# A top-256 search in an RWKV-7 and sparse-attention block: scratch room, conversions and fixed places for evictions

## The chip, the cores and the metric

The kernel runs on one core of a Trainium2 chip. A core has five engines that work side by side, each through its own queue in order: TensorE (PE, with its weight loads PEld), VectorE (DVE), ScalarE (ACT), GpSimd (POOL) and SyncE (SP), which issues the transfers. The metric is the device time of one execution in microseconds.

## The reference, cut to what matters

One block over T = 1024 tokens of width 1024. One projection of the normalised input feeds three parts: an RWKV-7 mixing, a sparse attention whose keys are picked by an indexer, and the gates that merge both; a feed-forward part follows. The change lies in the picking of the keys:

```
score  = einsum('bqh,bqhs->bqs', wi, relu(einsum('bqhd,bsd->bqhs', qi, ki)))
score  = where(causal, score, -inf)
_, idx = lax.top_k(score, 256)               # per query, over 1024 keys
s = where(valid, q . k[idx] / 8, -inf); p = softmax(s); out = p . v[idx]
z = token_shift(h @ w_in[rwkv columns], mu)  # z + (previous token's z - z) * mu
```

Queries go in eight blocks of 128. Blocks 0 and 1 have at most 256 keys and need no selection; block b has (b+1)*128 keys.

## The kernel before

The kernel has no gather. For each query it finds the 256th largest score exactly and writes a bias of 0 or -1e30 over the scores, which the attention adds. The scores are turned into integers of the same order and split into two int16 halves, `hi` and `lo`. `select` (L537 to L638) is a generator for three query blocks; two of them run, one for blocks 3, 4, 5 on ACT and one for blocks 2, 6, 7 on DVE, and L640 to L642 advance both in turn:

- *First half*: 16 steps of a bisection on `hi`. DVE (`bisect`) compares the 128 x n keys of each block with the candidate and counts in the same instruction, L577; two instructions of three columns make the next candidate. ACT (`bisect_signs`) takes the sign of key minus candidate and sums it, L590; POOL makes the next candidate, L592 to L598.
- *Conversion*, L605 to L615: `lo` becomes (hi - found) * 65536 + lo, clamped to int16. POOL does it for ACT's blocks (with a cast `low`), DVE for its own.
- *Second half*: the same 16 steps on the new `lo`.
- *Finals*, L616 to L638, on DVE for all six blocks: the threshold `thr`, `ge` (count), `eq`, a scan `cs` over the equal keys to break ties, two more passes and the bias.

The output of a comparison (`jk`) is junk; only its sum counts. These outputs and `q16`, `low`, `ge`, `eq`, `cs` and the attention's `hl` and `qs` all take slots of one ring of six tiles, tag `t4` (L352). A slot is free when the readers and writers of its last tenant are done, on whatever engine.

Beside the selection PE runs projections, each half (512 tokens) a run of 24 matmuls into a PSUM tile `dn` of a pool of two. First come the gates' (`gate1`, all pulled at L524, ACT evicts them at L452; the weights of the next unit are split by ACT L209 and POOL L210), then those of the RWKV part (`rin`): a half is 8 steps of that generator, and its eviction is a token shift by two engines: ACT L669 scales, DVE L670 adds the neighbour, ACT L673 or DVE L675 handles the column between the halves. 106 steps are pulled at L815 after the selection's code; then `q_split` makes `hl` (ACT L421, POOL L422) and PE transposes it (L430) for the first attention block, whose scores go through DVE at L774.

The order on each engine is made by a scheduler when the kernel is built: it goes by the program's order, dependencies and its own estimates. `after(first, ins)` (L175) adds a dependency that only fixes an order. So an eviction stands where the scheduler puts it between the comparisons.

Of the kernel before, what the change touches and what calls it, by code (L numbers as in the profile page):

```python
# [23 lines left out]
P = 128  # L24
# [9 lines left out]
NEG = -3.0e38  # L34
BIG = 1.0e30
PE_WINDOW = 32
FILL = [8, 2, 40, 3, 6, 22]
AHEAD = [6, 6, 6, 0, 0, 0, 0, 0, 1, 1, 0, 10]
FIN_LAG = 5
# [56 lines left out]
def hybrid_block(ctx: ExitStack, tc: tile.TileContext, a, out, dbg=None, stop=99):  # L96
# [78 lines left out]
    def after(first, ins):  # L175

        tc.add_manual_dep(ins.ins, first.ins.name, mybir.DependencyInfo(
            mybir.DependencyClass.NoSync, mybir.DependencyReason.DATA), reason="order of a queue")
# [20 lines left out]
    def pull(gen, n):  # L199
        for _ in range(n):  # L200
            if next(gen, "end") == "end":
                return
# [149 lines left out]
    def t4(name, dtype=F32):  # L352
        return dsa.tile([P, 1024], dtype, name=name, tag="t4", bufs=6)
# [176 lines left out]
    def t4b(name, n, dtype):  # L530
        return t4(name).bitcast(dtype)[:, 0:n]
# [5 lines left out]
    def select(blocks, act=False):  # L537
# [5 lines left out]
        def sm_(name, dtype=F32):  # L543
            return dsa.tile([P, m_], dtype, name=f"{name}{gi}")

        hi, lo = {}, {}
        room, o = None, 4096
        for b in reversed(blocks):
            n = (b + 1) * P
            if o + 2 * n > 4096:  # L550
                room, o = (key_room() if n > 384 else dsa.tile([P, 768], I16, name="room2")), 0
            hi[b], lo[b] = room[:, o:o + n], room[:, o + n:o + 2 * n]
            o += 2 * n
# [18 lines left out]
        def bisect(src):  # L572
            nc.vector.memset(cand, 0.0)
            for k in range(15, -1, -1):
                for j, b in enumerate(blocks):
                    junk = t4b("jk", (b + 1) * P, BF16)
                    nc.vector.tensor_scalar(junk, src[b], cand[:, j:j + 1], None, op0=OP.is_ge, op1=OP.add,  # L577
                                            accum_out=cnt[:, j:j + 1])
                up, down = step_of(k)
                nc.vector.tensor_scalar(ok, cnt, float(TOPK), up, op0=OP.is_ge, op1=OP.mult)  # L580
                nc.vector.scalar_tensor_tensor(cand, ok, -down, cand, op0=OP.add, op1=OP.add)
                yield

        def bisect_signs(src):
# [16 lines left out]

        search = bisect_signs if act else bisect
        yield from search(hi)
        th, tl = sm_("th"), sm_("tl", I32)
        eng.tensor_copy(th, cand)  # L605
        for j, b in enumerate(blocks):
            n = (b + 1) * P
            q = t4("q16")[:, 0:n]
            eng.tensor_scalar(q, hi[b], th[:, j:j + 1], 65536.0, op0=OP.subtract, op1=OP.mult)
            low = lo[b]  # L610
            if act:
                low = t4("low")[:, 0:n]
                eng.tensor_copy(low, lo[b])
            eng.tensor_tensor(q, q, low, op=OP.add)
            eng.tensor_scalar(lo[b], q, 32767.0, -32768.0, op0=OP.min, op1=OP.max)  # L615
        yield from search(lo)  # L616
        thr, ti = sm_("thr"), sm_("ti", I32)
        nc.vector.tensor_copy(ti, th)
        nc.vector.tensor_scalar(ti, ti, 16, None, op0=OP.logical_shift_left)
        nc.vector.tensor_scalar(tl, cand, 32768.0, None, op0=OP.add)  # L620
        nc.vector.tensor_tensor(ti, ti, tl, op=OP.bitwise_or)
# [15 lines left out]
            nc.vector.scalar_tensor_tensor(cs, sc[b], t_ap, cs, op0=OP.is_gt, op1=OP.add)  # L637
            nc.vector.tensor_scalar(sc[b], cs, BIG, -BIG, op0=OP.mult, op1=OP.add)  # L638

    searches = [select(blocks, act) for blocks, act in SELECT]  # L640
    while searches:
        searches = [g_ for g_ in searches if next(g_, "end") != "end"]  # L642
    if "bias" in dbg:
        for b in range(NB):
            nc.sync.dma_start(dbg["bias"][b * P:(b + 1) * P, 0:(b + 1) * P], sc[b])


    zd = dram.tile([4, P, 5, T], F32, name="zd")
# [13 lines left out]
    def shifted(c0, m, mkey, mi, fin):  # L662
        z = ev4()[0:m]
        last = base.tile([P, 1], F32, name="last", tag="last", bufs=2)[0:m]
        m0, m1 = pcol(mkey, mi)[0:m], pcol1(mkey, mi)[0:m]

        def evac(hf, ps):
            o = hf * 512
            nc.scalar.activation(z[:, o:o + 512], ps, AF.Copy, scale=m1)  # L669
            nc.vector.scalar_tensor_tensor(z[:, o + 1:o + 512], ps[:, 0:511], m0, z[:, o + 1:o + 512],  # L670
                                           op0=OP.mult, op1=OP.add)
            if hf == 0:
                nc.scalar.activation(last, ps[:, 511:512], AF.Copy)  # L673
            else:
                nc.vector.scalar_tensor_tensor(z[:, 512:513], last, m0, z[:, 512:513], op0=OP.mult, op1=OP.add)  # L675
                fin(z)

        yield from in_b(c0, m, evac)
# [7 lines left out]
    def split_lr(z, n):  # L686
        w = dsa.tile([P, 2, 1024], F32R, name="lrt", tag="room", bufs=2)
        nc.scalar.activation(w[0:n, 0, :], z, AF.Copy)
        nc.gpsimd.tensor_tensor(w[0:n, 1, :], z, w[0:n, 0, :].bitcast(F32), op=OP.subtract)
        return w  # L690

    def rwkv_in():
        keep = []
# [118 lines left out]
            nc.sync.dma_start(yt_dram[1, :, :, b * P:(b + 1) * P].rearrange("c p t -> p c t"), yT)  # L812

    rin = rwkv_in()
    pull(rin, RIN[0] - QF)  # L815
    A["hl"] = q_split(0, 0)
    pull(rin, QF)
    units = [(b, p) for b in range(NB) for p in range(4)]
# [774 lines left out]
    def in_order(ins):  # L1593
        if queue:
            after(queue[-1], ins)
        queue.append(ins)
# [154 lines left out]
```

## Time and profile before

| what | value |
|---|---|
| median of three runs | 1817.76 us (1809.3 to 1817.8) |
| profiled execution | 1819.81 us, span 1818.0 |
| mean granted TensorE clock | 0.959 |
| PE busy | 1697.3 us, 93% of the span |
| DVE busy | 1320.5 us, 73% |
| ACT, POOL busy | 895.2 us, 833.7 us |
| matmuls L189 into `dn` | 379.5 us in 1488 |
| DVE comparisons L577 | 92.6 us in 96, 15.1 idle before them |
| ACT comparisons L590 | 78.4 us in 96, 33.4 idle before them |

The profile follows one execution. Busy times are shares of the span of 1818.0 us; the profiled time has 1.8 us more. Times in the views count from the span's start; "A <- B" reads "A waited for B". A granted clock of 1.00 is 2.4 GHz, 0.50 is 1.2 GHz. Idle time of an engine costs only where something later waits for it.

### The profile page before, as it was taken

The numbers are of one execution on the slowest core, as the hardware profiler recorded it, in microseconds if no ns is written. First come the engines' busy times: TensorE is split into PE (matmuls) and PEld (weight loads), VectorE is DVE, ScalarE is ACT, GpSimd is POOL, SyncE is SP. The second block draws the span as 40 slices with busy tenths as digits, with TensorE's granted clock in tenths as the row PEclk, the third lists the DMA queues.
The fourth block names the chain that finished last, engine by engine and source line by source line (L and its number), as shares of the span: only waits on it lengthen the run. The fifth ranks groups of instructions, "written<-read, shape, count | busy, mean of one in ns | idle before, by whom it ended". The sixth has DMA issues, their size and how long they took to land.

```text
span 1818.0 us, 27188 instructions
## 1 busy us (share of the span) xinstructions
PE 1697.3 (93%) x9554; PEld 1424.4 (78%) x9554; DVE 1320.5 (73%) x2601; ACT 895.2 (49%) x1751; POOL 833.7 (46%) x761
## 2 busy tenths in 40 slices
PE   6999899849999999989898898999999999999997
PEld 6988887738788777777777797977888888888885
DVE  5689955996777454578666746699988875874988
ACT  5375664717777534245435425463444444444453
POOL 1522566324353334243423532286666656545552
PEclk9999999969999998799878999999999999999999
DMA  5230343212311355336436559415544549653444
GB/s 170 79 116 30 115 141 110 64 41 85 123 35 36 134 138 151 84 109 172 121 88 183 158 159 327 127 53 186 172 147 141 177 145 329 186 162 99 141 148 140
DMA packets 268287, 242.04 MB, mean 133 GB/s; under 512 B 64284, under 2 KB 206934, under 8 KB 268150
## 3 DMA queue, kind: packets, MB, share of 16 engines
q1 hardware_dynamic: 268150, 240.30, 42.3%
q8 instruction: 75, 1.23, 0.3%
q14 instruction: 62, 0.51, 0.1%
HBM read 164.76 MB, written 75.50 MB: 132 GB/s over the span
## 4 chain that ended last, share of the span: by engine, by line
PE 61%; DVE 18%; DMA 6%; POOL 4%; ACT 4%; issue 4%; SPq 1%; POOLq 0%; DVEq 0%; ACTq 0%
PE up L189 24%; PE dn L189 15%; PE sm L189 9%; DVE jk L577 3%; PE sm L192 2%; PE ch L189 2%; PE acc L189 2%; PE dn L243 1%; PE dn L244 1%; DVE w L1328 1%; PE dn L242 1%; DVE Zt L998 1%; PE acc L243 1%; POOL h L1328 1%; PE acc L242 1%
## 5 line engine op out<-in xcount | busy, mean ns | idle before, releaser
L189 PE MATMUL dn<-hT,w 128*128 128x512 f32 (+1 forms) x1488 | 379.5, 402 | 8.3 <-ACT last L673 7.5
L189 PEld LDWEIGHTS dn<-hT,w 128*128 128x128 f32 (+1 forms) x1488 | 274.0, 189 | 67.5 <-ACT last L673 10.1
L189 PE MATMUL up<-h,w 128*128 128x512 f32 x1344 | 312.1, 393 | 6.4 <-DVE w L1328 3.1
L189 PEld LDWEIGHTS up<-h,w 128*128 128x128 f32 x1344 | 252.3, 189 | 63.3 <-DVE w L1328 5.0
L1328 DVE TENSOR_TENSOR w<-st,w 128x512 fp32r<-128x512 f32 x216 | 213.5, 1022 | 75.6 <-ACT w L1327 75.5
L210 POOL TENSOR_TENSOR w<-st,w 128x1024 fp32r<-128x1024 f32 (+2 forms) x75 | 179.7, 2397 | 164.6 <-ACT w L209 139.1
L189 PE MATMUL up<-w 128*128 128x512 f32 x1008 | 246.1, 390 | 2.7 <-DVE w L1328 2.7
L189 PEld LDWEIGHTS up<-w 128*128 128x128 f32 x1008 | 188.6, 188 | 44.5 <-DVE w L1328 5.4
L1327 ACT ACTIVATE w<-st 128x512 fp32r<-128x512 f32 x216 | 127.9, 624 | 158.3 <-PE up L189 49.7
L1621 POOL TENSOR_TENSOR st<-wb,wb 128x512 f32<-128x512 f32 x80 | 120.7, 1512 | 93.9 <-DVE w L1328 73.8
L1483 POOL TENSOR_TENSOR c<-st 128x512 f32<-128x512 f32 x80 | 124.6, 1565 | 52.0 <-DMA st<-in_w_ffn_up 26.2
L209 ACT ACTIVATE w<-st 128x1024 fp32r<-128x1024 f32 (+2 forms) x91 | 94.7, 1041 | 42.0 <-PE acc L244 15.0
L577 DVE TENSOR_SCALAR_CACHE_REDUCE jk<-room,cand 128x384 bf16<-128x384 int16 (+2 forms) x96 | 92.6, 1008 | 15.1 <-ACT jk L590 14.1
L1494 POOL TENSOR_TENSOR C<-C 128x512 f32<-128x512 f32 x64 | 75.5, 1180 | 59.1 <-ACT C L1493 59.1
L243 PE MATMUL dn<-w,hT 128*128 128x256 f32 (+1 forms) x320 | 92.1, 289 | 6.3 <-DVE w L210 6.3
L780 POOL TENSOR_SCALAR sm<-sm,rs 128x128 f32<-128x128 f32 (+7 forms) x64 | 47.8, 748 | 105.1 <-DVE rs L779 55.2
L590 ACT ACTIVATE jk<-room,neg 128x512 bf16<-128x512 int16 (+2 forms) x96 | 78.4, 819 | 33.4 <-POOL neg L598 21.8
L242 PE MATMUL dn<-w,hT 128*128 128x256 f32 (+1 forms) x320 | 92.0, 290 | 0.9 <-ACT hT L272 0.9
L244 PE MATMUL dn<-w,hT 128*128 128x256 f32 (+1 forms) x320 | 92.0, 290 | 0.0
L1328 DVE TENSOR_TENSOR w<-c,w 128x512 fp32r<-128x512 f32 x80 | 82.7, 1046 | 0.4
L189 PE MATMUL sm<-w 128*128 128x512 f32 x288 | 81.1, 389 | 0.0
L1327 ACT ACTIVATE w<-c 128x512 fp32r<-128x512 f32 x80 | 48.8, 627 | 64.4 <-PE up L189 52.0
(336 smaller groups left out, 3546.3 us busy)
## 6 DMA issues: line engine op xcount, KB each, us to landing
st<-hcd SPq DMA_DIRECT2D x112, 256.0 KB
st<-in_w_in SPq DMA_DIRECT2D x54, 512.0 KB
st<-in_w_ffn_up SPq DMA_DIRECT2D x36, 512.0 KB
hcd<-C SPq DMA_DIRECT2D x16, 1024.0 KB
wb<-in_w_ffn_down SPq DMA_DIRECT2D x64, 256.0 KB
hcd<-kc SPq DMA_DIRECT2D x16, 768.0 KB
zd<-ev SPq DMA_DIRECT2D x20, 512.0 KB
gzd<-ev SPq DMA_DIRECT2D x32, 256.0 KB
```

The lines of the kernel that those rows point to most:

```text
L189: pe(nc.tensor.matmul(*args, **kw))
L209: nc.scalar.activation(hi, st[0:rows, 0:n], AF.Copy)
L210: (eng or nc.gpsimd).tensor_tensor(lo, st[0:rows, 0:n], hi.bitcast(F32), op=OP.subtract)
L242: nc.tensor.matmul(ps, l[0], r[0], start=start, stop=False, skip_group_check=shared)
L243: nc.tensor.matmul(ps, l[0], r[1], start=False, stop=False, skip_group_check=shared)
L244: nc.tensor.matmul(ps, l[1], r[0], start=False, stop=stop, skip_group_check=shared)
L577: nc.vector.tensor_scalar(junk, src[b], cand[:, j:j + 1], None, op0=OP.is_ge, op1=OP.add, accum_out=cnt[:, j:j + 1])
L590: nc.scalar.activation(junk, src[b], AF.Sign, bias=neg[:, j:j + 1], accum_out=cnt[:, j:j + 1])
L1327: nc.scalar.activation(hi, src, AF.Copy)
L1328: return eng.tensor_tensor(lo, src, hi.bitcast(F32), op=OP.subtract)
L1483: nc.gpsimd.tensor_tensor(c, src, blocks[LEFT[p][2]], op=OP.add if LEFT[p][1] == "+" else OP.subtract)
L1621: nc.gpsimd.tensor_tensor(c, src, wblocks[RIGHT[p][2], f], op=OP.add if RIGHT[p][1] == "+" else OP.subtract)
```

## The change

- DVE's comparisons get a tile of their own for their junk, outside the ring.
- Both conversions are on DVE; the cast `low` is dropped (DVE reads int16 directly).
- More `yield`s: DVE's second half stands in the program after both conversions.
- `in_order` ties DVE's first comparison of each step, its last instruction, the conversions, the finals' start and the evictions L670 (now L674) into one fixed order.
- The steps of `rin` are pulled in the selection's loop, by the numbers in `SPREAD`: eight (one half, one eviction) after each of eight turns of the second half, none after the others. The remaining 42 of the 106 follow after the loop.

```diff
+SPREAD = [0, 0, 0, 0, 0, 8, 8, 8, 8, 0, 8, 8, 8, 0, 8]
...
+        jk = None if act else dsa.tile([P, 1024], BF16, name="jk")
...
-                    junk = t4b("jk", (b + 1) * P, BF16)
-                    nc.vector.tensor_scalar(junk, src[b], cand[:, j:j + 1], None, op0=OP.is_ge, op1=OP.add,
-                                            accum_out=cnt[:, j:j + 1])
+                    ins = nc.vector.tensor_scalar(jk[:, 0:(b + 1) * P], src[b], cand[:, j:j + 1], None,
+                                                  op0=OP.is_ge, op1=OP.add, accum_out=cnt[:, j:j + 1])
+                    if j == 0:
+                        in_order(ins)
...
-                nc.vector.scalar_tensor_tensor(cand, ok, -down, cand, op0=OP.add, op1=OP.add)
+                own["V"] = nc.vector.scalar_tensor_tensor(cand, ok, -down, cand, op0=OP.add, op1=OP.add)
...
         yield from search(hi)
+        if act:
+            yield
...
-            eng.tensor_scalar(q, hi[b], th[:, j:j + 1], 65536.0, op0=OP.subtract, op1=OP.mult)
-            low = lo[b]
-            if act:
-                low = t4("low")[:, 0:n]
-                eng.tensor_copy(low, lo[b])
-            eng.tensor_tensor(q, q, low, op=OP.add)
-            eng.tensor_scalar(lo[b], q, 32767.0, -32768.0, op0=OP.min, op1=OP.max)
+            nc.vector.tensor_scalar(q, hi[b], th[:, j:j + 1], 65536.0, op0=OP.subtract, op1=OP.mult)
+            nc.vector.tensor_tensor(q, q, lo[b], op=OP.add)
+            own["V"] = in_order(nc.vector.tensor_scalar(lo[b], q, 32767.0, -32768.0, op0=OP.min, op1=OP.max))
+        if not act:
+            yield
         yield from search(lo)
         thr, ti = sm_("thr"), sm_("ti", I32)
-        nc.vector.tensor_copy(ti, th)
+        in_order(nc.vector.tensor_copy(ti, th))
...
+    own = {}
+
+    def in_order(ins):
+
+        if "V" in own:
+            after(own["V"], ins)
+        return ins
...
+            ins = in_order(nc.vector.scalar_tensor_tensor(z[:, o + 1:o + 512], ps[:, 0:511], m0,
+                                                          z[:, o + 1:o + 512], op0=OP.mult, op1=OP.add))
+            if searching[0]:
+                own["V"] = ins
...
     rin = rwkv_in()
-    pull(rin, RIN[0] - QF)
+    searches = [select(blocks, act) for blocks, act in SELECT]
+    searching[0], turn, early = True, 0, 0
+    while searches:
+        searches = [g_ for g_ in searches if next(g_, "end") != "end"]
+        n_ = SPREAD[turn - 19] if 19 <= turn < 19 + len(SPREAD) else 0
+        pull(rin, n_)
+        early += n_
+        turn += 1
+    searching[0] = False
...
+    pull(rin, RIN[0] - QF - early)
```

Where the order moves, first on ACT at the end of the first half. `jk` is a comparison, `ev` the eviction of a gate's half, `w` a weight split. Before, the last two steps and what follows:

```order
L590 ACTIVATE jk,cnt_2712<-room,neg_2716 128x512
L590 ACTIVATE jk,cnt_2712<-room,neg_2716 128x640
L452 ACTIVATE ev<-dn 128x512
L209 ACTIVATE w<-st 128x1024
L590 ACTIVATE jk,cnt_2712<-room,neg_2716 128x768
L452 ACTIVATE ev<-dn 128x512
L209 ACTIVATE w<-st 128x1024
L590 ACTIVATE jk,cnt_2712<-room,neg_2716 128x512
L590 ACTIVATE jk,cnt_2712<-room,neg_2716 128x640
L590 ACTIVATE jk,cnt_2712<-room,neg_2716 128x768
L452 ACTIVATE ev<-dn 128x512
L209 ACTIVATE w<-st 128x1024
```

After, the last two steps (lines are numbered as in the changed kernel; L452, L209 and L590 are now L453, L210 and L593):

```order
L593 ACTIVATE jk,cnt_2715<-room,neg_2719 128x512
L593 ACTIVATE jk,cnt_2715<-room,neg_2719 128x640
L593 ACTIVATE jk,cnt_2715<-room,neg_2719 128x768
L593 ACTIVATE jk,cnt_2715<-room,neg_2719 128x512
L593 ACTIVATE jk,cnt_2715<-room,neg_2719 128x640
L453 ACTIVATE ev<-dn 128x512
L210 ACTIVATE w<-st 128x1024
L593 ACTIVATE jk,cnt_2715<-room,neg_2719 128x768
L453 ACTIVATE ev<-dn 128x512
L210 ACTIVATE w<-st 128x1024
L453 ACTIVATE ev<-dn 128x512
L210 ACTIVATE w<-st 128x1024
```

Counted from the search's start, the evictions in the first piece are the eighth, ninth and tenth, those in the second the seventh to ninth: the sixteenth step's last comparison stands behind the ninth before and behind the seventh now. Four more gate evictions stand ahead of the second half before; now two do, and four stand within it.

On DVE, from the last step of the first half to the second half (`th` the found value, `q` the conversion, `room` the halves). Before, where the cast of `th_3031` is that of ACT's blocks, which DVE needs for the finals only:

```order
L581 SCALAR_TENSOR_TENSOR cand_2738<-ok_2739,cand_2738 128x3
L605 COPY th_3063<-cand_2738 128x3
L573 MEMSET cand_2738 128x3
L618 CAST ti_3398<-th_3063 128x3
L619 TENSOR_SCALAR ti_3398<-ti_3398 128x3
L618 CAST ti_3359<-th_3031 128x3
L619 TENSOR_SCALAR ti_3359<-ti_3359 128x3
L670 SCALAR_TENSOR_TENSOR ev<-dn,par,ev 128x511
L609 TENSOR_SCALAR q_3066<-room_2721,th_3063 128x384
L609 TENSOR_SCALAR q_3070<-room,th_3063 128x896
L609 TENSOR_SCALAR q_3074<-room,th_3063 128x1024
L614 TENSOR_TENSOR q_3066<-q_3066,room_2721 128x384
```

After, the end of the second conversion and the start of the second half:

```order
L614 TENSOR_SCALAR q_3009<-room,th_3002 128x640
L614 TENSOR_SCALAR q_3013<-room,th_3002 128x768
L615 TENSOR_TENSOR q_3005<-q_3005,room 128x512
L615 TENSOR_TENSOR q_3009<-q_3009,room 128x640
L615 TENSOR_TENSOR q_3013<-q_3013,room 128x768
L616 TENSOR_SCALAR room<-q_3005 128x512
L616 TENSOR_SCALAR room<-q_3009 128x640
L616 TENSOR_SCALAR room<-q_3013 128x768
L578 TENSOR_SCALAR jk,cnt_2741<-room_2725,cand_2742 128x384
L578 TENSOR_SCALAR jk,cnt_2741<-room,cand_2742 128x896
L578 TENSOR_SCALAR jk,cnt_2741<-room,cand_2742 128x1024
L583 TENSOR_SCALAR ok_2743<-cnt_2741 128x3
```

Before, the conversion of DVE's own blocks stands behind that cast and the first eviction of `rin` (L670). Now nine instructions for ACT's blocks stand behind its own nine, and no eviction is ahead of the second half.

Also on DVE, the place of the first eviction in the second half now, behind the seventh step:

```order
L578 TENSOR_SCALAR jk,cnt_2741<-room_2725,cand_2742 128x384
L578 TENSOR_SCALAR jk,cnt_2741<-room,cand_2742 128x896
L578 TENSOR_SCALAR jk,cnt_2741<-room,cand_2742 128x1024
L583 TENSOR_SCALAR ok_2743<-cnt_2741 128x3
L584 SCALAR_TENSOR_TENSOR cand_2742<-ok_2743,cand_2742 128x3
L674 SCALAR_TENSOR_TENSOR ev<-dn,par,ev 128x511
L578 TENSOR_SCALAR jk,cnt_2741<-room_2725,cand_2742 128x384
L578 TENSOR_SCALAR jk,cnt_2741<-room,cand_2742 128x896
L578 TENSOR_SCALAR jk,cnt_2741<-room,cand_2742 128x1024
L583 TENSOR_SCALAR ok_2743<-cnt_2741 128x3
L584 SCALAR_TENSOR_TENSOR cand_2742<-ok_2743,cand_2742 128x3
L674 SCALAR_TENSOR_TENSOR ev<-dn,par,ev 128x511
```

The next one follows one step later, and so on by `SPREAD`.

On DVE in the finals, before, from the first scan of a 768-wide block on:

```order
L633 SCALAR_TENSOR_TENSOR cs<-eq 128x768
L631 TENSOR_SCALAR ge,cnt_2737<-sc_1163,thr_3397 128x384
L636 SCALAR_TENSOR_TENSOR cs<-cs,gen_3366,eq 128x640
L638 TENSOR_SCALAR sc_1164<-cs 128x512
L634 SCALAR_TENSOR_TENSOR gen_3366<-cs,cnt_2712 128x1
L632 TENSOR_SCALAR eq<-sc_1163,thr_3397 128x384
L637 SCALAR_TENSOR_TENSOR cs<-sc_1165,thr_3358,cs 128x640
L636 SCALAR_TENSOR_TENSOR cs<-cs,gen_3366,eq 128x768
L633 SCALAR_TENSOR_TENSOR cs<-eq 128x384
```

After, at the same place:

```order
L636 SCALAR_TENSOR_TENSOR cs<-eq 128x768
L640 SCALAR_TENSOR_TENSOR cs<-sc_1164,thr_3516,cs 128x512
L634 TENSOR_SCALAR ge,cnt_2741<-sc_1163,thr_3555 128x384
L639 SCALAR_TENSOR_TENSOR cs<-cs,gen_3524,eq 128x640
L674 SCALAR_TENSOR_TENSOR ev<-dn,par,ev 128x511
L681 SCALAR_TENSOR_TENSOR ev<-last,par,ev 128x1
L637 SCALAR_TENSOR_TENSOR gen_3524<-cs,cnt_2715 128x1
L641 TENSOR_SCALAR sc_1164<-cs 128x512
L635 TENSOR_SCALAR eq<-sc_1163,thr_3555 128x384
```

There is one eviction (with its column L675) in the finals before, ahead of this piece; now six stand there, of which one is shown.

## Rows read from the trace of the kernel before

**Rows 1.** PE's waits from 284 to 405: waited for, us in total, times, longest

```profile
PE sm L430 <- POOL hl L422: 26.0, 1, 26.0
PE dn L189 <- ACT last L673: 7.5, 6, 2.5
```

**Rows 2.** A window: busy us of PE, PEld, DVE, ACT, POOL; granted clock, DMA

```profile
380.00:400.00 20.00, 0.87 (x4) 0.88 (x5) 20.00 (x31) 0.63 (x1) 3.72 (x1) 0.50 0.06 26
```

**Rows 3.** ACT's waits from 284 to 405

```profile
ACT hl L421 <- DVE cs L636: 23.5, 1, 23.5
```

**Rows 4.** DVE's timeline: start, us, operation, [idle before <-releaser]

```profile
261.68 0.19 DVE L605 COPY th<-cand 128x3 f32<-128x3 f32 x1
...
291.24 3.39 DVE L609 TENSOR_SCALAR q<-room,th 128x384 f32<-128x384 int16 x3
...
301.55 0.61 DVE L577 TENSOR_SCALAR_CACHE_REDUCE jk<-room,cand 128x384 bf16<-128x384 int16 x1
...
304.87 0.61 DVE L577 TENSOR_SCALAR_CACHE_REDUCE jk<-room,cand 128x384 bf16<-128x384 int16 x1
...
370.09 0.75 DVE L631 TENSOR_SCALAR_CACHE_REDUCE ge<-sc,thr 128x512 f32<-128x512 f32 x1
...
393.93 0.62 DVE L636 SCALAR_TENSOR_TENSOR cs<-cs,gen,eq 128x384 f32<-128x384 f32 x1
...
403.08 0.28 DVE L774 CUSTOM_DVE_ANT_0 sm<-acc,sc 128x128 f32<-128x128 f32 x1
```

**Rows 5.** DVE's waits from 160 to 292

```profile
DVE ev L670 <- ACT ev L669: 22.5, 1, 22.5
DVE jk L577 <- ACT jk L590: 14.1, 10, 3.0
```

**Rows 6.** POOL's timeline

```profile
267.09 0.19 POOL L605 COPY th<-cand 128x3 f32<-128x3 f32 x1
...
290.76 2.39 POOL L210 TENSOR_TENSOR w<-st,w 128x1024 fp32r<-128x1024 f32 x1
...
365.91 0.20 POOL L600 TENSOR_SCALAR cand<-neg 128x3 f32<-128x3 f32 x1
```

**Rows 7.** DVE's conversion from 286 to 302 by form: busy, mean ns, idle before

```profile
L609 DVE TENSOR_SCALAR q<-room,th 128x384 f32<-128x384 int16 x1 | 2.1, 2129 | 0.0
...
L609 DVE TENSOR_SCALAR q<-room,th 128x1024 f32<-128x1024 int16 x1 | 0.7, 741 | 0.0
...
L614 DVE TENSOR_TENSOR q<-q,room 128x1024 f32<-128x1024 f32 x1 | 1.2, 1214 | 0.0
...
L615 DVE TENSOR_SCALAR room<-q 128x1024 int16<-128x1024 f32 x1 | 0.7, 686 | 0.0
```

**Rows 8.** ACT's timeline

```profile
250.72 0.60 ACT L452 ACTIVATE ev<-dn 128x512 f32<-128x512 f32 x1 [1.72 <-PE dn L189]
...
252.16 0.71 ACT L590 ACTIVATE jk<-room,neg 128x512 bf16<-128x512 int16 x1
...
255.90 0.72 ACT L590 ACTIVATE jk<-room,neg 128x512 bf16<-128x512 int16 x1 [1.21 <-POOL neg L598]
...
261.60 0.60 ACT L452 ACTIVATE ev<-dn 128x512 f32<-128x512 f32 x1 [1.72 <-PE dn L189]
...
284.41 0.60 ACT L452 ACTIVATE ev<-dn 128x512 f32<-128x512 f32 x1 [4.90 <-issue]
...
299.82 0.72 ACT L590 ACTIVATE jk<-room,neg 128x512 bf16<-128x512 int16 x1 [2.93 <-DVE room L615]
```

**Rows 9.** PE's timeline (a row groups matmuls of one form)

```profile
244.62 33.71 PE L189 MATMUL dn<-hT,w 128*128 128x512 f32 x148
...
399.13 1.97 PE L430 MATMUL sm<-cst,hl 128*128 128x128 f32 x8 [26.00 <-POOL hl L422]
```

**Rows 10.** DVE's projection evictions from 301 to 410 by form

```profile
L670 DVE SCALAR_TENSOR_TENSOR ev<-dn,par,ev 128x511 f32<-128x511 f32 x13 | 9.7, 747 | 0.2 <-ACT ev L669 0.2
L675 DVE SCALAR_TENSOR_TENSOR ev<-last,par,ev 128x1 f32<-128x1 f32 x6 | 3.5, 576 | 0.0
```

More of the change, by code (lines that the diff above doesn't have):

```diff
@@ L638, in select @@
             nc.vector.tensor_scalar(sc[b], cs, BIG, -BIG, op0=OP.mult, op1=OP.add)
[L640 to L645, printed above, removed]
+    own = {}
[3 more added lines that the diff above has]
+        return ins
     zd = dram.tile([4, P, 5, T], F32, name="zd")
@@ L669, in evac @@
             nc.scalar.activation(z[:, o:o + 512], ps, AF.Copy, scale=m1)
-            nc.vector.scalar_tensor_tensor(z[:, o + 1:o + 512], ps[:, 0:511], m0, z[:, o + 1:o + 512],
-                                           op0=OP.mult, op1=OP.add)
+            ins = in_order(nc.vector.scalar_tensor_tensor(z[:, o + 1:o + 512], ps[:, 0:511], m0,
+                                                          z[:, o + 1:o + 512], op0=OP.mult, op1=OP.add))
+            if searching[0]:
+                own["V"] = ins
             if hf == 0:
@@ L690, in split_lr @@
         return w
+    searching = [False]
     def rwkv_in():
@@ L814, in hybrid_block @@
     rin = rwkv_in()
-    pull(rin, RIN[0] - QF)
+    searches = [select(blocks, act) for blocks, act in SELECT]
[7 more added lines that the diff above has]
+    searching[0] = False
+    if "bias" in dbg:
+        for b in range(NB):
+            nc.sync.dma_start(dbg["bias"][b * P:(b + 1) * P, 0:(b + 1) * P], sc[b])
+    pull(rin, RIN[0] - QF - early)
     A["hl"] = q_split(0, 0)
```

## Prediction

> **What bounds the kernel now.** I read the 40-slice table first: TensorE (PE) is busy 93% of the span, so only a stretch in which PE waits can give time. The waits of PE between 284 and 405 us show the largest single one: the transposes of the first attention block (L430) stand 26.0 us, and six waits for ACT's evictions add 7.5 [rows 1]. In the table of windows PE is busy 0.87 of the 20 us from 380 to 400, and its granted clock there is 0.50, the lower of its two levels (1.2 of 2.4 GHz) [rows 2]. The waits of ACT name what is behind it: POOL makes `hl` (L422) from ACT's L421, and this one stands 23.5 us for DVE's `cs` L636 in the finals [rows 3], since `hl` takes a slot of the ring of six that all of selection's scratch uses. So PE has run out of work that may be done before attention, and attention needs the end of selection, which DVE reaches at 403.08 with its first attention operation [rows 4]. What ends selection earlier is worth its full length until PE is busy throughout. DVE itself was not short of time before: its waits show 14.1 us in ten waits for ACT's junk outputs in the first half and one wait of 22.5 us for the eviction L669 [rows 5], at the end of which its conversion begins, at 291.24 [rows 4]. The second half starts at 301.55 only.
>
> **Part 1, the start of the second half.** Three things hold it at 301.55, and all three are edited.
>
> (a) *DVE's comparisons in the ring.* Ten waits, 14.1 us, go [rows 5]. This is worth nothing by itself: DVE's first half, over at 261.68 before [rows 4], ends some 14 us sooner, near 247.5, but the second half now stands behind the threshold of ACT's blocks too. What is late next is that threshold, at 267.09 [rows 6]. DVE's own conversion fits in between. Its clean price at 1024 columns is 0.74+1.21+0.69=2.64 us [rows 7]; its blocks have 2304 columns, so 2.64 x 2304/1024 = 5.9 us, done by about 254 to 256.
>
> (b) *ACT's first half.* In ACT's old order the 16th step stands behind the ninth gate eviction (261.60), in the new one its last comparison stands behind the seventh (250.72) [rows 8]. These evictions come at PE's pace: 148 matmuls take 33.71 us, 0.228 each, so 24 for one half are 5.47 [rows 9]. Two halves are 10.9 us: the threshold would come at 256. ACT's own pace is the other bound: a bare step is 252.16 to 255.90, 3.74 us [rows 8], and the new order gives some weight splits later, which may let PE wait 1 to 2 us. I take 259, between 256 and 267 (unchanged).
>
> (c) *The conversion of ACT's blocks.* On POOL it came between the threshold at 267.09 and the weight split at 290.76 [rows 6], with other splits inside. On DVE it is 1920 columns: 2.64 x 1920/1024 = 5.0 us, 5.2 with nine fixed parts. It adds 9 instructions to DVE and takes 12 from POOL, whose L592 to L600 thus no longer stand behind it. A price against it: DVE's first conversion, L609 at 384 columns, took 2.13 us where the 1024 wide one took 0.74 [rows 7]; it began at 291.24 and so ended at 293.37, when POOL's split of 290.76 had just ended at 293.15 [rows 4, 6]. Such an operation is up to 2.13-0.74 = 1.4 us longer here, and at most by a split's 2.4. Splits come once per half (5.47 us), so the 11 us of both conversions meet about two: bounds 0 and 2 x 2.4 = 4.8; I take 1, near the row. The Trainium skill ("SBUF — State Buffer", section "Who interferes with whom") has a rule that speaks against moving work to DVE here: DVE and GpSimd share one port pair, whoever issues first holds it for the whole instruction, and `tensor_scalar` without accumulator is among the forms that take it. The row agrees; by the rule the upper bound of 4.8 is the likelier one, and the second half would start 4 us later than the sum has it. The second half then starts at 259+5.2+1 = 265 (262 to 274), against 301.55: 36 us earlier.
>
> **Part 2, the second half.** A step of DVE is 304.87-301.55 = 3.32 us [rows 4]; sixteen are 53.1. The pinned order puts the first projection eviction behind the seventh step: 265+23 = 288. PE's halves come anyway later: the last gate eviction was at 284.41 [rows 8], the next half 5.47 behind, with PE's slip 291. So DVE waits there about 3 us, which is also the cover for a second half that starts up to 3 us late. Eight evictions lie in the half, each 0.75 plus every second time 0.58 [rows 10], 8.3 together; at PE's pace the eighth comes at 291+7x5.47 = 329. By its own work alone DVE would be through at 265+53.1+8.3 = 326; PE's pace sets 330. ACT: 16 bare steps are 59.8; before, the fifteen from 299.82 to the last threshold at 365.91 took 66.1 [rows 8, 6], 4.4 a step with evictions and splits in them, so 16 take 70.5. That gives 325 to 336; I take 335, near the measured pace. The finals' first `ge` then comes some 4 us later (365.91 to 370.09 before, [rows 6, 4]): 339 in place of 370.09, 31 us earlier. SP's output transfers of these projections go with the same evictions at PE's pace, and PE's weights are asked for in the old order: nothing there.
>
> **Part 3, the finals.** From the first `ge` to the first attention operation DVE took 403.08-370.09 = 33.0 us with one eviction in it [rows 4]. The 42 remaining steps of the projections now lie in there, six evictions: five more, 5 x 0.75 + 3 x 0.58 = 5.5 us [rows 10]. Attention may start at 339+33+5.5 = 377.5: 25.5 earlier. `hl` gets its slot nine us ahead of that, as before (393.93 against 403.08), and so at 368; with ACT's and POOL's share, 399.13-393.93-0.62 = 4.6 us before [rows 4, 9], it is there at 373.
>
> **PE's side.** From 286 PE has 14 halves and a 14-matmul rest, 14 x 24 + 14 = 350 matmuls, 350 x 0.228 = 80 us: to 366, plus its waits for evictions, 7.5 before [rows 1], 8 to 10 now that order is fixed: 374 to 376. So of the 26.0 us little is left, and the transposes move from 399.13 [rows 9] to about 375: 24. PE and DVE agree within 1.5 us; the smaller, **24 us**, is the sum. All that follows (attention, RWKV, output) has nearly the same order and is PE-bound; some reshuffled stretches may give or take 5 us. That PE's clock need no longer fall to 0.50 [rows 2] is left as reserve.
>
> The profiled execution took 1819.8 (span 1818.0 and 1.8 around it): 1819.8-24 = 1795.8. It stood 2 us above the median of the runs, 1817.8: forecast **1794**.
>
> **Rivals.**
> *ACT's first half does not come earlier* (chance 0.15). For it: a third of ACT's bare step is waiting for POOL (1.21 of 3.74, [rows 8]), and the new order may only exchange one wait for another. This is also the case in which the change does not do what it says: (a) turns into waiting for ACT. Threshold 267, second half at 273, DVE by 334, ACT by 343.5, `ge` at 347, less the 5.5 in the finals: 17.5 earlier, so 1800. Against it: the order itself, and rows 8.
> *The finals become a chain of evictions* (0.14). Six of them now stand between `ge`, scan and `cs`, each needs PE's half and ACT's part first. If each holds DVE for 3 us (one wait of PE for that chain is at most 2.5, [rows 1]), 18 of the 24 go: 1812. Against it: PE's fourteenth half is ready at 291+13x5.47 = 362, long before the finals need it.
> *Slower: the second half falls into lockstep* (0.09). Every fixed eviction ties ACT, DVE and PE: if a step with an eviction takes the sum of DVE's 3.32+0.75, ACT's step without its wait 2.53 + 0.60, POOL's thresholds 1.21 and a split of 2.39 [rows 4, 6, 8, 10], that is 10.8 instead of 5.47, and eight cost 43 us against the gain of 24: 19 slower, 1837. It decides from 5.47+24/8 = 8.5 us per eviction on. Against it: ACT and DVE search different blocks, and two PSUM buffers lie between.
>
> **How the numbers follow.** The forecast has 0.62, its own range 1788 to 1801 (start of the second half 262 to 270, ACT's second half 60 to 76 us, 5 us behind). About 0.5%, 9 us, is what a measurement of this kernel can tell from no change: faster is below 1808.7, slower above 1826.9. Faster: 0.62+0.15 and 0.03 of the chained finals, **0.80**; same 0.11 of these and 0.01 of the lockstep, **0.12**; slower **0.08**. The range 1785 to 1811 holds most of the first, the second and half of the third case.
>
> **What would show it.** In the profile of after: DVE's waits for `jk` of ACT gone; ACT's 16th threshold near 259; first comparison of the second half near 265 (above 270 refutes Part 1b); DVE's first projection eviction near 291, the eighth near 330, and PE without waits above 3 us between; finals from about 339 and 38 us long; PE's wait before the transposes below 6 us; granted clock near 1.00 from 360 to 380; first attention operation near 378. DVE conversions of 2.4 us beside POOL's splits would bear out the port rule. If the attention starts 25 us earlier and the end does not, the later stretches took it back. Evictions more than 8.5 us apart would make the prediction wrong altogether.

## The result, and the profile after

The changed kernel takes 1791.07 us in the median of four runs (1784.69 to 1804.62); four runs of the kernel before on the same chip gave 1814.39. The ratio is 0.9894, 95% interval 0.9861 to 0.9926 (the two medians alone divide to 0.987). A second series of the unchanged pair gave 1786.61 against 1812.36, ratio 0.9865 (0.9845 to 0.9885). The forecast was 1794. The profiled execution took 1787.29 us, its span is 1785.5.

PE's waits from 250 to 400 us (waited for, us in total, times, longest), and the window from 380 to 400 with the granted clock third from the end, answer to [rows 1, 2]:

```profile
PE dn L190 <- ACT ev L453: 4.1, 1, 4.1
PE dn L190 <- DVE ev L674: 3.7, 2, 2.4
```

```profile
380.00:400.00 20.00, 17.50 (x94) 14.38 (x93) 12.65 (x48) 10.88 (x31) 8.60 (x10) 1.00 0.17 46
```

The wait of 26.0 us for `hl` is gone, and so is the lower clock: 17.50 us of matmuls stand where 0.87 did. What is left of PE's waiting is a few us for evictions. PE's transposes, which stood at 399.13 [rows 9]:

```profile
277.05 45.75 PE L190 MATMUL dn<-hT,w 128*128 128x512 f32 x192 [4.12 <-ACT ev L453]
...
376.29 1.03 PE L431 MATMUL sm<-cst,hl 128*128 128x128 f32 x8
...
377.56 3.48 PE L190 MATMUL dn<-hT,w 128*128 128x512 f32 x14 [0.24 <-ACT last L679]
```

DVE's timeline of the same stretch, for [rows 4] (start, duration, operation; names as before, lines up to eight higher):

```profile
253.08 0.17 DVE L610 COPY th<-cand 128x3 f32<-128x3 f32 x1
...
262.79 5.78 DVE L614 TENSOR_SCALAR q<-room,th 128x512 f32<-128x512 int16 x3 [3.81 <-POOL neg L589]
...
271.90 0.60 DVE L578 TENSOR_SCALAR_CACHE_REDUCE jk<-room,cand 128x384 bf16<-128x384 int16 x1
...
275.46 0.61 DVE L578 TENSOR_SCALAR_CACHE_REDUCE jk<-room,cand 128x384 bf16<-128x384 int16 x1
...
278.63 1.80 DVE L583 TENSOR_SCALAR ok<-cnt 128x3 f32<-128x3 f32 x1
...
299.70 0.75 DVE L674 SCALAR_TENSOR_TENSOR ev<-dn,par,ev 128x511 f32<-128x511 f32 x1
...
343.47 0.75 DVE L634 TENSOR_SCALAR_CACHE_REDUCE ge<-sc,thr 128x512 f32<-128x512 f32 x1
...
353.01 2.82 DVE L640 SCALAR_TENSOR_TENSOR cs<-sc,thr,cs 128x512 f32<-128x512 f32 x1
...
368.48 1.50 DVE L639 SCALAR_TENSOR_TENSOR cs<-cs,gen,eq 128x384 f32<-128x384 f32 x1
...
384.28 0.28 DVE L782 CUSTOM_DVE_ANT_0 sm<-acc,sc 128x128 f32<-128x128 f32 x1
```

The second half starts at 271.90 (before 301.55, forecast 265), the first `ge` stands at 343.47 (370.09; 339) and attention starts at 384.28 (403.08; 377.5). One step of DVE now takes 275.46-271.90 = 3.56 us, not 3.32. POOL's rows, for [rows 6], and the first conversion operations by form (busy, mean ns), for [rows 7]:

```profile
256.93 4.31 POOL L211 TENSOR_TENSOR w<-st,w 128x1024 fp32r<-128x1024 f32 x1 [3.17 <-ACT w L210]
...
262.57 0.18 POOL L610 COPY th<-cand 128x3 f32<-128x3 f32 x1
...
262.75 4.93 POOL L211 TENSOR_TENSOR w<-st,w 128x1024 fp32r<-128x1024 f32 x2
...
278.03 2.38 POOL L211 TENSOR_TENSOR w<-st,w 128x1024 fp32r<-128x1024 f32 x1 [3.17 <-ACT w L210]
...
336.29 0.20 POOL L603 TENSOR_SCALAR cand<-neg 128x3 f32<-128x3 f32 x1
```

```profile
L614 DVE TENSOR_SCALAR q<-room,th 128x640 f32<-128x640 int16 x1 | 2.7, 2684 | 0.0
L614 DVE TENSOR_SCALAR q<-room,th 128x512 f32<-128x512 int16 x1 | 2.6, 2647 | 3.8 <-POOL neg L589 3.8
...
L614 DVE TENSOR_SCALAR q<-room,th 128x768 f32<-128x768 int16 x1 | 0.6, 608 | 0.0
```

The two narrower operations took 2.65 and 2.68 us beside POOL's two splits from 262.75 to 267.68, the widest 0.61 after them. An operation of three columns, L583, took 1.80 us beside the split of 278.03, where the same line took 0.17 in the steps without one; both end at 280.4. In the other direction POOL's split of 256.93 took 4.31 us, not 2.4, beside DVE's own conversion, and ACT's threshold stood behind it.

### The profile page after: what moved, and what is told of

Its sections match the earlier page's. It is cut to its first block, busy times and chain, and to the rows that moved or that the text cites. A ratio compares the mean times of both kernels' runs of the same rounds, so it can differ in the third digit from the quotient of the medians.

```text
span 1785.5 us, 27137 instructions
## 1 busy us (share of the span) xinstructions
PE 1685.5 (94%) x9554; PEld 1415.8 (79%) x9554; DVE 1336.4 (75%) x2610; ACT 894.3 (50%) x1751; POOL 821.8 (46%) x749
## 4 chain that ended last, share of the span: by engine, by line
PE 56%; DVE 21%; DMA 7%; ACT 5%; issue 5%; POOL 4%; SPq 1%; POOLq 0%; DVEq 0%; ACTq 0%
PE up L190 24%; PE dn L190 11%; PE sm L190 9%; DVE jk L578 2%; PE sm L193 2%; PE ch L190 2%; DVE w L1348 2%; DMA zt<-zd 2%; PE acc L190 2%; PE dn L245 1%; PE dn L244 1%; PE dn L243 1%; ACT jk L593 1%; DVE LT L958 1%; DVE Z L1020 1%
## 5 line engine op out<-in xcount | busy, mean ns | idle before, releaser
L190 PEld LDWEIGHTS dn<-hT,w 128*128 128x128 f32 (+1 forms) x1488 | 274.1, 189 | 72.0 <-ACT ev L453 5.3
L211 POOL TENSOR_TENSOR w<-st,w 128x1024 fp32r<-128x1024 f32 (+2 forms) x75 | 183.3, 2445 | 186.8 <-ACT w L210 153.1
L210 ACT ACTIVATE w<-st 128x1024 fp32r<-128x1024 f32 (+2 forms) x91 | 94.6, 1041 | 46.6 <-PE acc L245 15.4
L578 DVE TENSOR_SCALAR_CACHE_REDUCE jk<-room,cand 128x384 bf16<-128x384 int16 (+2 forms) x96 | 97.1, 1012 | 2.9
L593 ACT ACTIVATE jk<-room,neg 128x512 bf16<-128x512 int16 (+2 forms) x96 | 78.5, 819 | 34.4 <-POOL neg L601 26.7
```

The source lines that it names most:

```text
L190: pe(nc.tensor.matmul(*args, **kw))
L210: nc.scalar.activation(hi, st[0:rows, 0:n], AF.Copy)
L211: (eng or nc.gpsimd).tensor_tensor(lo, st[0:rows, 0:n], hi.bitcast(F32), op=OP.subtract)
L578: ins = nc.vector.tensor_scalar(jk[:, 0:(b + 1) * P], src[b], cand[:, j:j + 1], None, op0=OP.is_ge, op1=OP.add, accum_out=cnt[:, j:j + 1])
L593: nc.scalar.activation(junk, src[b], AF.Sign, bias=neg[:, j:j + 1], accum_out=cnt[:, j:j + 1])
```

## The experiments

The change has three parts: the room (R), the conversion of ACT's blocks on DVE (C) and the fixed places (F). Eight kernels hold every combination. The table reads their traces at two points, the first comparison of DVE's second half and the first attention operation on DVE; the ratio is against the kernel before on the same chip.

| run | parts | second half | attention | ratio (95% interval) |
|---|---|---|---|---|
| before, e8 | none | 301.6, 300.1 | 403.1, 401.7 | 1.0017 (0.9996 to 1.0037) |
| e2 | R | 297.3 | 412.3 | 1.0031 (1.0015 to 1.0047) |
| e12 | F | 293.3 | 406.7 | 1.0014 (0.9996 to 1.0031) |
| e6 | R, F | 259.3 | 395.9 | 0.9963 (0.9948 to 0.9979) |
| e3 | C | 278.8 | 381.7 | 0.9865 (0.9839 to 0.9891) |
| e5 | R, C | 275.6 | 392.2 | 0.9932 (0.9902 to 0.9963) |
| e9 | C, F | 278.4 | 387.5 | 0.9871 (0.9834 to 0.9909) |
| after, e1 | R, C, F | 271.9, 272.4 | 384.3, 384.9 | 0.9894, 0.9865 |

In e6 the 259.3 is DVE's alone; ACT's second half starts at 287.1 there.

**e1, the changed kernel again**, no edit.

> The changed kernel once more, unchanged. The profile of after is 32.5 us shorter than that of before, but PE reaches the same matmul of the first attention block only 19 us earlier; the other 13 us come in stretches that the change does not touch. Theory (stage): the transposes L431 stand at 376 again, 19 us are the gain of the change, ratio near 0.989, and the stretch behind the transposes differs by some us from that of the first profile, with the granted clock. Rival (later stretches gain too): the stretch behind the transposes is 10 us or more shorter than before's again and the ratio is near 0.982.

Measured: transposes at 376.99, attention at 384.88, ratio 0.9865. The stretch repeats to 0.7 us. From attention to the end there are 1405.4 us, in the first profile of after 1401.2, against 1414.9 in before: 9.5 and 13.7 us less. The ratio lies between the theory's 0.989 and the rival's 0.982.

**e8, the kernel before again**, no edit.

> The kernel before once more, for a second profile. Behind the matmul of the first attention block its first profile had 1398 us, those of five other kernels 1382 to 1390. Theory (that stretch varies by the granted clock, whatever the kernel): 1382 to 1392 here, the transposes at 399 again, ratio 1.000. Rival (the old order makes the later stretches slower): 1396 or more again.

Measured: 1.0017, transposes at 397.70, attention at 401.65, and behind that 1414.9 us, as in the first profile (1818.0-403.1 = 1414.9). So the rival's number came. But this profile is of the slowest of the twelve executions, 1818.25 us against a median of 1810.19, and the first one, 1819.81 us, is slower than the four runs of before in the result. So up to 8 us of the 1414.9 can belong to these executions and not to the kernel. Over the other kernels this rest runs from 1397 to 1410 without a link to a part: e2, which gains nothing, has 1399.8, e5 1410.2. The mean granted clock from 430 to 1300 us is 0.94 and 0.93 in the two profiles of before and 0.93 to 0.96 in all others. Whether the old order as such makes the rest slower stays open; by the rows in front of attention the change is worth 17 to 19 us, by the ratios of the two series 19 and 24 (by their medians 23 and 26).

**e2, the room alone.**

```diff
+        jk = None if act else dsa.tile([P, 1024], BF16, name="jk")
...
-                    junk = t4b("jk", (b + 1) * P, BF16)
-                    nc.vector.tensor_scalar(junk, src[b], cand[:, j:j + 1], None, op0=OP.is_ge, op1=OP.add,
+                    nc.vector.tensor_scalar(jk[:, 0:(b + 1) * P], src[b], cand[:, j:j + 1], None, op0=OP.is_ge, op1=OP.add,
```

> The kernel before with the tile of its own for DVE's comparisons and nothing else. Theory (stage): DVE no longer waits for ACT's slots, ACT's threshold comes near 262 in place of 267, but POOL's conversion (23 us) and the first projection eviction still stand ahead of the second half: it starts near 292 to 295 in place of 301.6, the transposes come 6 to 9 us earlier, ratio 0.995 to 0.997. Rival (the room carries the gain): second half near 272, ratio 0.989. Second rival (worth nothing, as the prediction said of it alone): ratio 1.000.

Measured: 1.0031, slower by 0.3%, which neither the theory nor a rival had. DVE's waits from 250 to 375, ACT's from 270 to 375 and PE's from 250 to 410:

```profile
DVE q L609 <- POOL room L615: 23.3, 1, 23.3
```

```profile
ACT last L673 <- DVE ev L670: 19.8, 5, 5.6
```

```profile
PE sm L430 <- POOL hl L422: 21.4, 1, 21.4
```

The wait for ACT's slots turned into one of 23.3 us for POOL's conversion, whose tiles fill the ring that DVE's conversion needs too. And the scheduler now puts evictions into the middle of steps: ACT's column copy waits 19.8 us for DVE's evictions, and with it ACT's second half lasts from 285.5 to 373.4 (start of the first to start of the last comparison), 88 us in place of 75.

**e3, the conversion alone**: `eng.` becomes `nc.vector.` in its three operations, the cast goes; nothing else.

```diff
-            eng.tensor_scalar(q, hi[b], th[:, j:j + 1], 65536.0, op0=OP.subtract, op1=OP.mult)
-            low = lo[b]
...
+            nc.vector.tensor_scalar(q, hi[b], th[:, j:j + 1], 65536.0, op0=OP.subtract, op1=OP.mult)
+            nc.vector.tensor_tensor(q, q, lo[b], op=OP.add)
```

> The kernel before with both conversions on DVE and nothing else: comparisons stay in the ring, evictions go where the scheduler puts them. Theory (stage): ACT's threshold stays near 267, the conversions take 9 us, the second half starts near 276 and the transposes come 13 to 17 us earlier: ratio 0.991 to 0.993, so most of the change's gain. Rival (fixed places carry it): without them the evictions hold DVE up or starve PE, and no more than 5 us are gained, ratio 0.997 or more.

Measured: 0.9865, as much as the whole change in the same series and more than the theory's 0.991 to 0.993; the transposes come at 377.4, 21.7 us earlier than before. DVE's second half starts 7 us later than in after (278.8), but its steps are 3.32 us and the scheduler lets the first eviction come behind the fourth step (DVE's timeline; L666 is the eviction here), and PE's wait before the transposes is 4.0 us. The first three operations on ACT's blocks ran beside no split; the three-column cast behind them did (POOL's split of 267.36), and took 2.39 us:

```profile
266.00 1.48 DVE L609 TENSOR_SCALAR q<-room,th 128x512 f32<-128x512 int16 x3 [5.03 <-POOL neg L586]
267.39 2.39 DVE L614 CAST ti<-th 128x3 int32<-128x3 f32 x1
...
278.78 0.60 DVE L577 TENSOR_SCALAR_CACHE_REDUCE jk<-room,cand 128x384 bf16<-128x384 int16 x1
...
282.10 0.61 DVE L577 TENSOR_SCALAR_CACHE_REDUCE jk<-room,cand 128x384 bf16<-128x384 int16 x1
...
293.30 0.75 DVE L666 SCALAR_TENSOR_TENSOR ev<-dn,par,ev 128x511 f32<-128x511 f32 x1 [0.61 <-ACT ev L665]
```

```profile
PE sm L430 <- POOL hl L422: 4.0, 1, 4.0
```

One thing moves with the conversion here: in the kernel before, the scheduler puts the first eviction ahead of DVE's conversion, where DVE waits 22.5 us for it [rows 5]; in e3 it puts it into the second half. So e3 by itself does not tell the engine of the conversion from that place; e6 does.

**e4, no step of the projections in the loop.**

```diff
-SPREAD = [0, 0, 0, 0, 0, 8, 8, 8, 8, 0, 8, 8, 8, 0, 8]
+SPREAD = [0, 0, 0, 0, 0, 0, 0, 0, 0, 0, 0, 0, 0, 0, 0]
```

> The changed kernel with all numbers of the table zero: no projection step is pulled in the search's loop, all evictions stand behind the search on DVE. Theory (stage): the search ends earlier (first ge near 330 in place of 343) but PE stands from about 302, when two halves fill its two buffers, to about 328: some 25 us; twelve halves are left then, 66 us, and the transposes come near 394 to 400, so the gain is all but gone: ratio 0.997 to 1.003. Rival (evictions inside the second half are worth little): the finals' start alone decides, transposes near 370, ratio 0.986.

Measured: 1.0022 (1.0005 to 1.0039), attention at 407.0. PE's waits from 250 to 410:

```profile
PE dn L190 <- DVE ev L674: 36.3, 3, 33.7
```

The second half starts at 271.9 as in after, but PE stands 33.7 us with both buffers full. The search ends near 332, yet the first `ge` comes at 354.9, not 330: three evictions stand ahead of it, for which DVE waits 17 us. The whole gain goes: pinned evictions have to stand in the second half once the order is pinned.

**e5, room and conversion, free places**: the edits of e2 and e3 together.

> The kernel before with the tile of its own and both conversions on DVE, without fixed places: the scheduler places the evictions. Theory (conversion alone carries the gain; the room makes the scheduler put evictions into the middle of DVE's steps, where they wait, and the fixed places only repair that): second half near 272, first eviction after seven steps and a half near 300, later ones inside steps, transposes 380 to 390, ratio 0.989 to 0.994, worse than the conversion alone (0.9865). Rival (the three parts add up, and the fixed places are the smallest): transposes near 372 to 376, ratio 0.984 to 0.987.

Measured: 0.9932; the first eviction comes at 304.4, behind seven steps and three comparisons, and PE's waits for evictions sum to 18.9 us. The room costs here, beside the same conversion.

**e6, the changed kernel with the conversion of ACT's blocks on POOL.**

```diff
+            if act:
+                low = t4("low")[:, 0:n]
+                nc.gpsimd.tensor_scalar(q, hi[b], th[:, j:j + 1], 65536.0, op0=OP.subtract, op1=OP.mult)
+                nc.gpsimd.tensor_copy(low, lo[b])
+                nc.gpsimd.tensor_tensor(q, q, low, op=OP.add)
+                nc.gpsimd.tensor_scalar(lo[b], q, 32767.0, -32768.0, op0=OP.min, op1=OP.max)
+                continue
```

> The changed kernel with the conversion of ACT's three blocks back on POOL; room, fixed places and DVE's own conversion stay. Theory (conversion carries the gain): ACT's threshold near 262, POOL converts until about 285, ACT's second half 285 to 355, DVE's own second half starts near 259 and waits at its first fixed eviction; first ge near 358, transposes near 390, ratio 0.995 to 1.001. Rival (fixed places carry it and rescue this too): transposes near 378, ratio below 0.990.

Measured: 0.9963, transposes at 392.0 behind a wait of 21.3 us for `hl`. ACT's blocks end the search, as the theory had it. Against after only the conversion's engine (with its cast) differs, and all evictions have the same fixed places: on POOL attention starts 11.7 us later.

**e12, the fixed places alone**: e6 with the comparisons back in the ring.

> The fixed places alone: the changed kernel with DVE's comparisons back in the ring and the conversion of ACT's blocks back on POOL. It is the last of the eight combinations of the three parts. Theory (the conversion's engine decides): POOL's conversion ends near 285 again, ACT's second half starts there, first attention operation at 398 or later, ratio 0.997 to 1.006. Rival (each part gives a share): first attention operation near 392, ratio 0.990 to 0.994.

Measured: 1.0014, attention at 406.7. POOL's conversion ends at 295.0, not 285. DVE's second half waits for it in the ring, the first fixed eviction comes at 322.1, and PE stands for it, not for `hl`:

```profile
DVE jk L577 <- POOL room L618: 23.7, 1, 23.7
```

```profile
PE dn L190 <- ACT last L685: 26.8, 2, 26.5
```

**e9, conversion and fixed places, without the room.**

> The changed kernel with DVE's comparisons back in the ring: conversion on DVE and fixed places stay, the room goes. Theory (conversion alone carries the gain, fixed places neither add nor cost beside the ring): ACT's threshold near 265, second half near 277, steps of 3.32 us as in the conversion alone, transposes 375 to 381, ratio 0.985 to 0.990. Rival (the fixed places need the early second half that the room gives, so without it evictions come late): transposes at 385 or later, ratio 0.993 or more.

Measured: 0.9871; transposes at 380.1, attention at 387.5. Attention starts 5.8 us later than in e3, but in the times the fixed places neither add nor cost what these runs can tell.

**e7, another form of the conversion.**

```diff
-            nc.vector.tensor_scalar(q, hi[b], th[:, j:j + 1], 65536.0, op0=OP.subtract, op1=OP.mult)
-            nc.vector.tensor_tensor(q, q, lo[b], op=OP.add)
+            nc.vector.tensor_scalar(q, hi[b], th[:, j:j + 1], None, op0=OP.subtract, op1=OP.add,
+                                    accum_out=cnt[:, j:j + 1])
+            nc.vector.scalar_tensor_tensor(q, q, 65536.0, lo[b], op0=OP.mult, op1=OP.add)
```

> The changed kernel with another form of the conversion: the difference as a tensor_scalar with accumulator, the factor 65536 moved into a scalar_tensor_tensor with lo, the clamp as before; so the first of the three operations is the form that DVE runs as its comparisons, which in no trace were stretched by POOL's splits. Theory (a shared port holds tensor_scalar without accumulator): the first three operations on ACT's blocks, 5.78 us beside two splits in after, take 2.4 to 2.6 us, POOL's split of 256.9 takes 2.4 in place of 4.3 where only the difference runs beside it, the second half starts near 269 in place of 271.9; at most 3 us come off the end, ratio against before 0.984 to 0.987. Rival (the stretch was something else, or moves to the scalar_tensor_tensor, which reads two tiles): second half at 271 or later.

Measured, DVE from 250 to 276 by form (busy, mean ns):

```profile
L616 DVE SCALAR_TENSOR_TENSOR q<-q,room 128x512 f32<-128x512 f32 x1 | 2.9, 2853 | 0.0
...
L614 DVE TENSOR_SCALAR_CACHE_REDUCE q<-room,th 128x512 f32<-128x512 int16 x1 | 0.7, 747 | 0.6 <-POOL neg L589 0.6
...
L616 DVE SCALAR_TENSOR_TENSOR q<-q,room 128x640 f32<-128x640 f32 x1 | 0.8, 811 | 0.0
```

The accumulating form ran in 0.75 us while POOL's splits were on, where the plain form took 2.65; the operation behind it, which reads two tiles, took 2.85 in place of the 0.68 of after's L615 of the same width. The stretch moved. The second half starts at 270.1, 1.8 us earlier, between the theory's 269 and the rival's 271, and attention at 384.0. The ratio is 0.9969 (0.9951 to 0.9986), 11 us worse than attention's start would have it. The profiled execution, 1794.3 us, is the fastest of the twelve (median 1802.5) and does not show why; this stays open.

**e10, three tiles for the junk, and e11, places one step earlier.**

```diff
-        jk = None if act else dsa.tile([P, 1024], BF16, name="jk")
+        jk = None if act else [dsa.tile([P, (b + 1) * P], mybir.dt.uint8, name=f"jk{b}") for b in blocks]
...
+SPREAD = [0, 0, 0, 0, 8, 8, 8, 0, 8, 8, 8, 0, 8, 8, 8]
```

The last line is e11's alone.

> The changed kernel with three tiles of one byte for the junk of DVE's three blocks in place of one tile of two bytes, every comparison pinned as the first is now. Theory (each comparison into the one tile waits 0.12 us for the one before it: a step of 3.56 us, against 3.32 in the ring): step 3.32 again, the second half 16 x 0.24 = 4 us shorter where PE does not pace it, first ge near 340 in place of 343.5, transposes 1 to 3 us earlier, ratio 0.984 to 0.988. Rival (the 0.12 us comes from the accumulator's reading, not from the tile): step stays 3.56.

> The same with other fixed places: first eviction behind the sixth step in place of the seventh, nine in the second half in place of eight. Theory (at 299.7 the first eviction came some 6 us after PE had the half ready near 295, and later ones make PE wait): first eviction near 293, PE waits 3 to 5 us less before the transposes, which come near 371 to 373; ratio 0.982 to 0.986, the fastest of all. Rival (ACT's step then waits for more evictions and its threshold comes later): transposes at 376 or later, ratio as e10.

Measured: 0.9889 (0.9848 to 0.9929) and 0.9859 (0.9825 to 0.9893), attention at 386.4 and 384.2. DVE's timeline of e10:

```profile
276.07 0.61 DVE L578 TENSOR_SCALAR_CACHE_REDUCE jk<-room,cand 128x384 uint8<-128x384 int16 x1
276.60 0.08 DVE L578 DVE_READ_ACCUMULATOR jk<-room,cand 128x1 f32 x1
276.60 1.14 DVE L578 TENSOR_SCALAR_CACHE_REDUCE jk<-room,cand 128x896 uint8<-128x896 int16 x1
...
279.39 0.61 DVE L578 TENSOR_SCALAR_CACHE_REDUCE jk<-room,cand 128x384 uint8<-128x384 int16 x1
```

A step is 3.32 us again, so the 0.24 came from the one tile. But with the new room the scheduler reordered the first half: ACT's threshold comes at 250.4, and DVE's first half lasts until 265.4. The second half starts at 276.1 and the 4 us are gone. In e11 the first eviction came at 299.5, not 293, since its second half, too, starts later (274.1), and ACT's gate evictions make PE wait 9.3 us. No version beats the conversion alone or the whole change by what these runs can tell.

## Why the prediction was right, and where it was off

**The bound was right.** PE's wait for `hl` fell from 26.0 to nothing, and with it 17 to 19 us in front of attention; that this stretch sets the time is shown from the other side by e4, where 33.7 us of waiting elsewhere take the gain back.

**Part 1a, the room is worth nothing by itself, held** (e2: 1.0031), but for a reason that the prediction had not named: the wait reappears as one of DVE's conversion for the ring (23.3 us), and the scheduler answers with other places. DVE's first half ended at 253.08, not 247.5; sixteen steps of 3.56 in place of 3.32 us (Part 2) are 3.8 of that.

**Part 1b, the threshold of ACT's blocks at 259, came at 262.6.** The order gave the two halves, but a split of POOL now stands ahead of the threshold, and it was stretched by DVE's own conversion, 4.31 in place of 2.4 us: 1.9 of the 3.6 us. The port rule of the Trainium skill ("SBUF — State Buffer", section "Who interferes with whom") speaks of both engines; the sum had costed only DVE's side.

**Part 1c, the conversion, was mis-sized**: 5.2+1 us were taken, 271.90-262.79 = 9.1 measured. The three first operations took 5.78 us where e3's same three, beside no split, took 1.48: 4.3 us of stretch, beside an upper bound of 4.8. So the bound, and the later start that the port rule gave, were nearer than the 1 us taken. The same section of the Trainium skill excepts the accumulating form and counts forms that read two tiles among those that are held; e7 agrees with both, 0.75 and 2.85 us.

**Part 2, the step of 3.32 us, failed as well**: one tile for three comparisons makes it 3.56 (e10). Seven steps are 24.9 in place of 23.2, and three of their seven operations L583 were held by POOL's splits (1.80, 0.79 and 0.73 us in place of 0.17), 2.8 us more, which no term of the sum had. So the first eviction came 27.8 us behind the start, at 299.7, not 291, and the eighth at 341.8, not 330. PE's second buffer covered the first; PE ran 192 matmuls from 277.05 without a wait. What it waited for was a gate's eviction on ACT, 4.1 us, which stands in ACT's second step of the second half and so behind the conversion. The forecast said that a second half above 270 would refute Part 1b; it was 271.9, 3.6 us from the threshold and 2.9 from the conversion.

**Part 3 and PE's side.** The second half started 6.9 us late, the first `ge` only 4.5, since ACT's second half took 65.1 us (271.21 to its threshold at 336.29) where 70 were taken. The finals took 384.28-343.47 = 40.8 us, forecast 38.5. The transposes came at 376.3, forecast 375; but they no longer show the end, since 14 matmuls stand behind them. DVE's end decides, 384.3 in place of 377.5: a gain of 17 to 19 in place of 24. By the ratios the runs gained 19 and 24 us (intervals 13 to 25 and 21 to 28). What they gained beyond 17 to 19, nothing to 7 us, lies behind attention's start (e8) and is not explained. That the median came within 3 us of 1794 is thus in part luck: a stretch that gained less than summed, and a rest that gained where the sum had nothing.

**The credit was given to the wrong parts.** The prediction valued the fixed places and ACT's earlier first half as steps of one sum. In the table of the eight combinations the conversion on DVE brings attention forward by 12 to 21 us beside each of the four settings of the other two parts; with it the ratios are 0.9865 to 0.9932, without it 0.9963 to 1.0031. The room alone puts attention back by 9.2 us and the fixed places alone by 3.6; together they bring it 7.2 forward without the conversion (e6) and put it 2.6 back beside it (e3 to after). What the conversion on POOL held up stands in the profile of before:

```profile
267.38 2.00 POOL L609 TENSOR_SCALAR q<-room,th 128x512 f32<-128x512 int16 x1
...
288.35 2.33 POOL L615 TENSOR_SCALAR room<-q 128x512 int16<-128x512 f32 x3
```

```profile
289.00 0.72 ACT L590 ACTIVATE jk<-room,neg 128x512 bf16<-128x512 int16 x1 [3.04 <-POOL room L615]
```

ACT's second half starts behind these 23.3 us. Three weight splits are 7.2 of them and the casts 2.2, too little for dropping the cast to carry the gain; a conversion on POOL without it was not run. Starting the second half 7 us earlier than e3 brings nothing by these rows: in after PE runs without a pause from 277.05 to 322.8, so the halves come at its pace.

**The rivals.** The slower one, lockstep, did not come in after, where the places are fixed between steps; it came in part in e2, where the scheduler chose them: three gaps between evictions are 10.8 to 11.6 us there, the others 4.1 to 7.3. The chain of evictions in the finals did not come: DVE waited for none of them. What is 2.3 us above the forecast fits the holds: four operations beside POOL's work ran 5.5 us longer in the finals than clean ones (L640 took 2.82 us, where before's L637 of that form took 0.75), in before two ran 3.2 us longer. The unchanged threshold came half true (262.6 between 259 and 267).

## What to carry to other kernels

When several engines share one ring of scratch tiles, look for the slow operation behind which the others wait: here POOL's conversion, 23 us with the splits between its parts, for what DVE does in 7 to 9 (e3, after). Move that one first and time it alone; more room for the others only moves the wait. Before an operation goes to DVE, read what POOL runs at that moment, and cost the hold in both directions.

## What the runs showed of the hardware

- Of three comparisons into one tile the second and third start 0.12 us later than into tiles of their own or of the ring: 3.56 against 3.32 us a step (after, e10).
- DVE and POOL held each other for about a whole operation: two `tensor_scalar` of 512 and 640 columns took 2.65 and 2.68 us, so that three took 5.78 in place of 1.48 (after, e3), and POOL's split 4.31 in place of 2.40. Operations of three columns were held as long: 1.80 in place of 0.17 us (after), 2.39 for a cast (e3). The accumulating form ran beside the split in 0.75 us (e7), the time of before's `ge` of that form and width.
- The stretch behind attention's start varied from 1397 to 1415 us over 14 profiles, with the granted clock of 430 to 1300 us between 0.93 and 0.96: as much as the change itself.
